# Splitting the second halves of K's and V's weights at later places in the recurrence

## Chip, cores and metric

The kernel runs as one program on one core of a Trainium2 chip. The metric is the device time of one execution in microseconds (us). The kernel before takes 1784.86 us, the median of three runs (1783.5 to 1788.74).

## What is computed

The reference is one inference step of a two-layer encoder over 544 tokens (512 of a prompt, 32 of a sample). Layer 0 is an RWKV-7 layer of 32 heads of 64, layer 1 a stick-breaking attention. The change touches layer 0 alone, cut here to what matters:

```python
h, gate = ada_modulate(x, c, norm_g, ada_w, ada_b)
r, k, v, z = split(concat([h, dx]) @ concat([w_in, w_mu]))      # four projections 1024 -> 2048
def step(s, inp):                                               # per token and head, s is 64 x 64
    s_kk = einsum('bhvk,bhk->bhv', s, kk_t)
    s = s * w_t - s_kk * (kk_t * a_t) + v_t * k_t
    return s, einsum('bhvk,bhk->bhv', s, r_t)
```

The projections K and V are what the moved instructions prepare weights for; the recurrence is computed in chunks of 64 tokens.

## The kernel before

**Tiling.** Activations lie with their features on the 128 partitions and the 544 tokens along the free dimension, in two halves of 272 tokens. A projection of 128 output columns multiplies eight 128x128 weight tiles with eight 128x272 activation tiles for each half. Float32 accuracy comes from splitting every operand into a rounded high part and a low remainder, and from three matmuls per tile (high by high, high by low, low by high).

**Weights.** `wfetch` (L219) loads half of one projection's weights (four of its eight tiles, 256 KB) into one of four raw buffers through the SyncE queue (SP). `wsplit` (L224) makes the high part `whi` by a copy on ScalarE (ACT, L231) and the low part `wlo` by a subtraction (L232), in the recurrence on VectorE (DVE). In the recurrence there are three pairs of `whi` and `wlo` buffers, used in turn; a split waits until the matmuls that read the buffer's last contents are done, and `wlo` waits for `whi`.

**Schedule.** The 2048 features are 16 pairs of heads. While pair p is prepared, pair p-2 runs its recurrence: one unit of the schedule ("an iteration" below) holds the V projection of one pair (places 0 to 0.5), the K projection of another (0.5 to 1), the recurrence of a third, and the vector work of others. The order on every engine is written out by hand: `at(t, fn)` enters a step at a place t, a table `SHIFT` moves some of them by thousandths, and `flush` (L530) issues all steps sorted by place. Each engine runs its own instructions in that order, so one that waits holds up all that stand behind it on the same engine. A projection issues 16 quanta of three matmuls, half by half (`quantum`, L553); 11/32 of an iteration after the start of its slot (less 0.0107 by the table) stands the last quantum that reads the first half of the weights.

**Order of the halves.** Per iteration four halves are split in the order K0, K1 (the K weights for the next slot) and V0, V1. With three buffers, K1 takes the buffer that V0 held, and V1 the one that K0 held. V0 is last read by the quantum at place 0.333, K0 by the one at 0.833; before the change K1 is split at place 0.300 and V1 at 0.800. K0 (0.22) and V0 (0.72) take the buffers of the projections that ended before.

**The chain of the recurrence** (`plan_c`, L887) is in eight steps n per iteration, at places 3n/24 (`x`), (3n+1)/24 (`u`) and (3n+2)/24 (`s`): L907 on TensorE (PE) multiplies the state, L918 copies on DVE, L929 on PE, L932 and L933 copy on ACT, L944 on PE, L952 on DVE makes the new state `st`, and L922 on ACT scales it. Step 2's `st` stands at 0.3333, step 6's at 0.8333. In front of step 2's on DVE stands also L666, which makes `rk`.

**The triangular inverses** (`plan_b`, L730): per iteration GpSimd (POOL) runs 31 pairs of instructions (L771, L776) on one pair of heads, each depending on the one before. Their input goes through DRAM: masks on DVE (L689), stores on SP (L741), loads into `npt` (L754); their result is stored by SP (L757) and fetched back (L745), and DVE transposes it (L791, place 0.86) for the matmuls of L797. On SP these stand in the order L741, L757 (which waits for POOL's last add), L754, L745.

Of the kernel before, what the change touches and what calls it, by code (L numbers as in the profile page):

```python
# [87 lines left out]
def tile_encoder(ctx: ExitStack, tc: tile.TileContext, i, o):  # L88
# [130 lines left out]
    def wfetch(n, kh):  # L219
        raw = wp.tile([P, KH, P], F32, tag="wraw", name="wraw", bufs=RBUF)  # L220
        SY.dma_start(raw, wsrc[n][kh * KH * P:(kh + 1) * KH * P].rearrange("(k p) c -> p k c", p=P))
        return raw

    def wsplit(raw):  # L224

        n, pool = wcount[0] % (WBUF + WMORE if wmore else WBUF), wp
        wcount[0] += 1
        if n >= WBUF:
            pool = wmore[0]
        hi, lo = (pool.tile([P, KH, P], F32R, tag=f"{nm}{n}", name=nm, bufs=1) for nm in ("whi", "wlo"))  # L230
        A.copy(hi, raw)  # L231
        (V if onV[0] else G).tensor_tensor(out=lo, in0=raw, in1=hi.bitcast(F32), op=ALU.subtract)  # L232
        return hi, lo
# [288 lines left out]
    def at(t, fn, *args):  # L522

        names = fn.__qualname__.split(".<locals>.")[1:]
        name = names[-1]
        alike = name in ("row", "add", "quantum", "x", "u", "s") or (name == "y" and args != (8,))
        key = " ".join([layer[0]] + names + [str(a) for a in args if not alike])
        agenda.append((t + SHIFT.get(key, 0.0), len(agenda), fn, args))
# [4 lines left out]
            fn(*args)  # L533
        agenda.clear()

    def plan_load(idx, t, d=0.17):

        parts = wready[idx] = [None, None]

        def load(kh):  # L540
            parts[kh] = wfetch(idx, kh)

        def split_w(kh):
            parts[kh] = wsplit(parts[kh])
        for kh in range(2):
            at(t + 0.3 * d * kh, load, kh)
            at(t + d + 0.47 * d * kh, split_w, kh)

    def plan_proj(x, idx, t0, t1, evac):

# [618 lines left out]
    at(1.02, open_b)  # L1169
    for p, q in enumerate(pairs):  # L1170
        if p >= 2:
            plan_load(q.kw, p - 0.95)
        if p >= 1:
            plan_load(q.vw, p + 0.55)
        for plan in (plan_a, plan_lm, plan_b, plan_m, plan_v, plan_c, plan_d):
            plan(q)

# [162 lines left out]
    for k in range(NK):  # L1340
# [14 lines left out]
        else:  # L1355
            t = p3.tile([P, T], F32, tag="t3", name="sqt", bufs=4)
# [65 lines left out]
    def plan_zb(j, idx, t0, t1):  # L1422

        st = {}

        def evac(half, ps, s):
            if half == 0:
                st["t"] = p4.tile([P, T], F32, tag="szb", name="szb", bufs=2)
            u = p4.tile([P, HT], F32, tag="nsq", name="sgm", bufs=2)
            A.activation(u, ps, AF.Sigmoid)  # L1430
            V.tensor_tensor(st["t"][:, s], ps, u, ALU.mult)
        plan_load(idx, t0 - 0.2, 0.1)
        plan_proj(xb, idx, t0, t1, evac)

        def store():
            SY.dma_start(sz_d[j], st["t"])
        at(t1 + 0.05, store)
# [358 lines left out]
```

## Time and profile before

| What | Value |
|---|---|
| median of 3 runs | 1784.86 us (1783.5 to 1788.74) |
| the profiled execution: time | 1785.67 us |
| the profiled execution: span, first to last instruction | 1784.0 us |
| busy in the span: PE, ACT, DVE, POOL | 94%, 50%, 43%, 38% |
| mean granted TensorE clock | 0.982 of full speed |
| the recurrence, start of its first step to the end of its last | about 256 to 875 us |

The profile is of one execution. Busy shares are of the whole span; the two granted levels of the TensorE clock are 1.2 and 2.4 GHz, and a mean between them is a mix of the two. The recurrence runs in 16 iterations (numbered 2 to 17 by the schedule's places); K1 is split in iterations 2 to 14 and V1 in 2 to 15. An iteration's bounds are taken as the starts of its first L907 matmul on `s`. Times in rows are from the start of the span.

### The profile page before, as it was taken

How to read it: one execution, taken by the hardware profiler on the slowest of the kernel's cores; microseconds unless marked ns; L12 is line 12 of the kernel's file. 1: busy time of each engine (PE TensorE's matmuls, PEld its weight loads, DVE VectorE, ACT ScalarE, POOL GpSimd, SP SyncE). 2: the span in 40 equal slices, each digit the busy share in tenths (PEclk: the TensorE clock that was granted, in tenths of full speed). 3: DMA queues.
4: the chain of work that ended last, by engine and by line, in shares of the span. 5: the costliest groups of instructions: out<-in, count | busy, mean ns of one | idle time of the engine just before them, and what ended most of it. 6: DMA issues, size and time to landing. Idle time of an engine off the chain costs nothing. (4 is left out here: it accounts for less than half of the span.)

```text
span 1784.0 us, 38442 instructions
## 1 busy us (share of the span) xinstructions
PE 1675.3 (94%) x15107; PEld 1444.3 (81%) x15107; DVE 765.6 (43%) x1564; ACT 884.9 (50%) x2232; POOL 681.4 (38%) x1371
## 2 busy tenths in 40 slices
PE   5999979999999999999989998999999999999899
PEld 2679867777777777778868998998888888888798
DVE  3674445545555545552355223123443434334400
ACT  2555545565565556555443335254554545555521
POOL 1000276656667666663002443432222222222432
PEclk8999989999999999989999999999999999999999
DMA  8457522333232333332585443433233232323232
GB/s 326 154 160 233 180 76 69 108 84 86 73 80 73 107 80 93 94 89 66 178 287 148 125 142 91 139 106 110 63 85 88 66 107 58 98 75 103 78 111 79
DMA packets 302612, 203.75 MB, mean 114 GB/s; under 512 B 79726, under 2 KB 271872, under 8 KB 300256
## 3 DMA queue, kind: packets, MB, share of 16 engines
q1 hardware_dynamic: 302432, 201.30, 38.2%
q8 instruction: 119, 1.95, 0.5%
q14 instruction: 61, 0.50, 0.1%
HBM read 155.28 MB, written 45.96 MB: 113 GB/s over the span
## 5 line engine op out<-in xcount | busy, mean ns | idle before, releaser
L560 PE MATMUL mm<-x,whi 128*128 128x272 f32 x3584 | 798.4, 315 | 7.0 <-DVE x L1274 3.5
L560 PEld LDWEIGHTS mm<-x,whi 128*128 128x128 f32 x3584 | 572.0, 191 | 70.7 <-issue 23.3
L232 POOL TENSOR_TENSOR wlo<-wraw,whi 128x512 fp32r<-128x512 f32 x198 | 255.2, 1299 | 702.1 <-ACT whi L231 702.1
L560 PE MATMUL mm<-x,wlo 128*128 128x272 f32 x1792 | 520.8, 291 | 1.7 <-POOL wlo L232 1.7
L560 PEld LDWEIGHTS mm<-x,wlo 128*128 128x128 f32 x1792 | 341.3, 190 | 2.4 <-POOL wlo L232 2.4
L231 ACT CAST whi<-wraw 128x512 fp32r<-128x512 f32 x324 | 195.1, 618 | 138.1 <-issue 78.4
L771 POOL TENSOR_TENSOR qtmp<-npt,qp 108x84 f32<-108x84 f32 (+23 forms) x496 | 194.0, 391 | 77.9 <-DMA npt<-nd_d 38.4
L776 POOL TENSOR_TENSOR qp<-qp,qtmp 108x84 f32<-108x84 f32 (+23 forms) x496 | 194.7, 393 | 37.9
L232 DVE TENSOR_TENSOR wlo<-wraw,whi 128x512 fp32r<-128x512 f32 x126 | 88.9, 707 | 116.3 <-ACT whi L231 114.6
L260 PE MATMUL mm<-x,whi 128*128 128x272 f32 x512 | 101.2, 293 | 2.8 <-POOL x L1733 1.4
L932 ACT COPY vu<-ch 64x64 f32<-64x64 f32 (+1 forms) x128 | 27.5, 215 | 133.7 <-PE ch L929 133.4
L952 DVE SCALAR_TENSOR_TENSOR st<-ch,gc,sgc 128x64 f32<-128x64 f32 x128 | 35.7, 279 | 128.2 <-PE ch L944 125.0
L260 PEld LDWEIGHTS mm<-x,whi 128*128 128x128 f32 x512 | 81.7, 190 | 3.9 <-POOL x L1733 1.8
L560 PE MATMUL mm<-xrh,whi 128*128 128x272 f32 x240 | 73.0, 304 | 1.6 <-ACT rout L1087 1.4
L260 PE MATMUL mm<-x,wlo 128*128 128x272 f32 x256 | 74.5, 291 | 0.0
L260 PE MATMUL mm<-yh,whi 128*128 128x272 f32 x256 | 73.9, 288 | 0.0
L260 PE MATMUL mm<-yh,wlo 128*128 128x272 f32 x256 | 73.8, 288 | 0.0
L260 PE MATMUL mm<-yl,whi 128*128 128x272 f32 x256 | 73.8, 288 | 0.0
L560 PE MATMUL mm<-xrh,wlo 128*128 128x272 f32 x240 | 69.3, 289 | 0.3 <-DVE wlo L232 0.3
L560 PE MATMUL mm<-xrl,whi 128*128 128x272 f32 x240 | 69.1, 288 | 0.0
L922 ACT ACTIVATE sgc<-st,gc 128x64 f32<-128x64 f32 x112 | 38.7, 346 | 46.6 <-DVE st L952 46.2
L1640 ACT ACTIVATE z<-z 128x512 f32<-128x512 f32 (+1 forms) x48 | 27.8, 579 | 68.1 <-DVE z L1637 68.1
(322 smaller groups left out, 3180.0 us busy)
## 6 DMA issues: line engine op xcount, KB each, us to landing
wraw<-in_a_w_in_dram SPq DMA_DIRECT2D x128, 256.0 KB
wraw<-in_kv_w_dram SPq DMA_DIRECT2D x68, 256.0 KB
wraw<-in_b_w_in_dram SPq DMA_DIRECT2D x64, 256.0 KB
rca<-rca_d SPq DMA_DIRECT2D x16, 816.0 KB
rca_d<-sgat SPq DMA_DIRECT2D x16, 544.0 KB
x<-in_a_ada_w_dram SPq DMA_DIRECT2D x8, 1024.0 KB
adaw<-in_b_ada_w_dram SPq DMA_DIRECT2D x8, 1024.0 KB
wraw<-in_a_w_out_dram SPq DMA_DIRECT2D x32, 256.0 KB
```

The source lines that it names most:

```text
L231: A.copy(hi, raw)
L232: (V if onV[0] else G).tensor_tensor(out=lo, in0=raw, in1=hi.bitcast(F32), op=ALU.subtract)
L260: TE.matmul(ps[:, :HT], a[:, k % KH, :], b[:, k, s], start=n == 0, stop=n == total - 1)
L560: TE.matmul(ps[half][:, :HT], a[:, k % KH, :], b[:, k, s], start=k + n == 0, stop=k == NK - 1 and n == 2)
L771: G.tensor_tensor(q.tt, q.npt[:, j, j + 1:32].unsqueeze(1).broadcast_to([108, ni, nt]), q.qp[:, 0:ni, j:j + 1].broadcast_to([108, ni, nt]) ...
L776: G.tensor_tensor(q.qp[:, 0:ni, j + 1:32], q.qp[:, 0:ni, j + 1:32], q.tt, ALU.add)
L922: A.activation(sg, state[c], AF.Copy, scale=q.gc[:, c:c + 1])
L932: A.copy(q.vu[64:128, cs, 0, :], pu[64:128, 0:64 * m].rearrange("p (m t) -> p m t", m=m))
L952: V.scalar_tensor_tensor(new, src, gc, ps["g", c], ALU.mult, ALU.add)
L1640: A.activation(z[b][:, :width[b]], z[b][:, :width[b]], AF.Exp)
```

## The change

`plan_load` gets an optional place for the split of the second half. For K it is p - 0.57 (place 0.43 of the iteration instead of 0.300), for V it is p + 0.895 (0.895 instead of 0.800). The loads, the first halves, the buffers and their order stay, and so do the other layer's calls of `plan_load`, which give no such place.

```diff
-    def plan_load(idx, t, d=0.17):
+    def plan_load(idx, t, d=0.17, second=None):
...
         for kh in range(2):
             at(t + 0.3 * d * kh, load, kh)
-            at(t + d + 0.47 * d * kh, split_w, kh)
+            at(second if kh and second else t + d + 0.47 * d * kh, split_w, kh)
...
         if p >= 2:
-            plan_load(q.kw, p - 0.95)
+            plan_load(q.kw, p - 0.95, second=p - 0.57)
         if p >= 1:
-            plan_load(q.vw, p + 0.55)
+            plan_load(q.vw, p + 0.55, second=p + 0.895)
```

## Rows read from the trace of the kernel before

**Rows 1.** The page: its span, and busy time, share and instructions by engine.
```profile
span 1784.0 us, 38442 instructions
PE 1675.3 (94%) x15107; PEld 1444.3 (81%) x15107; DVE 765.6 (43%) x1564; ACT 884.9 (50%) x2232; POOL 681.4 (38%) x1371
```

**Rows 2.** Stretches (us, busy by engine, PE clock, DMA): iterations 3-14, 10, 11.
```profile
295.75:756.83 461.08, 435.72 (x5515) 347.48 (x5513) 244.00 (x540) 267.42 (x794) 307.64 (x853) 0.99 0.33 85
563.67:603.26 39.59, 37.41 (x466) 29.89 (x464) 20.30 (x45) 22.30 (x68) 26.25 (x73) 0.96 0.31 81
603.26:641.24 37.98, 35.95 (x466) 28.64 (x463) 20.38 (x45) 22.28 (x68) 26.04 (x73) 1.00 0.33 85
```

**Rows 3.** Waits, 256 to 875 us: who for whom, us, times, longest.
```profile
PE ch L907 <- DVE st L952: 21.9, 17, 1.8
...
DVE wlo L232 <- ACT whi L231: 77.6, 44, 3.4
...
ACT whi L231 <- PE mm L560: 11.7, 27, 1.0
```

**Rows 4.** Timeline (start, us, what, [idle before]), iteration 10, K1; last: iteration 11.
```profile
574.34 0.50 DVE L1033 SCALAR_TENSOR_TENSOR yr<-yr,vecb,vs 128x272 f32<-128x272 f32 x1
...
575.41 0.62 ACT L231 CAST whi<-wraw 128x512 fp32r<-128x512 f32 x1 [0.51 <-PE mm L560]
...
575.42 0.34 PE L944 MATMUL ch<-vu,kbt 128*64 128x64 f32 x4
...
576.06 0.86 DVE L232 TENSOR_TENSOR wlo<-wraw,whi 128x512 fp32r<-128x512 f32 x1 [1.22 <-ACT whi L231]
...
576.85 0.86 DVE L666 TENSOR_TENSOR rk<-rca,k 128x544 f32<-128x544 f32 x1
577.63 0.27 DVE L952 SCALAR_TENSOR_TENSOR st<-ch,gc,sgc 128x64 f32<-128x64 f32 x1
...
577.96 0.33 PE L907 MATMUL ch<-st,ar 64*64 64x64 f32 x4 [1.51 <-DVE st L952]
...
617.37 0.33 PE L907 MATMUL ch<-st,ar 64*64 64x64 f32 x4 [1.33 <-DVE st L952]
```

**Rows 5.** Timeline, iteration 10 around V1's split.
```profile
597.03 0.69 DVE L232 TENSOR_TENSOR wlo<-wraw,whi 128x512 fp32r<-128x512 f32 x1 [3.10 <-ACT whi L231]
...
597.60 0.29 PE L560 MATMUL mm<-x,wlo 128*128 128x272 f32 x1
...
597.98 0.33 PE L907 MATMUL ch<-st,ar 64*64 64x64 f32 x4
...
599.33 0.34 PE L797 MATMUL aux<-mt,lm 32*32 32x32 f32 x10 [0.19 <-DVE mt L791]
```

**Rows 6.** Timeline, iteration 11 around place 0.43.
```profile
619.90 0.21 ACT L933 COPY vu<-ch 64x64 f32<-64x64 f32 x1
...
621.17 0.28 DVE L952 SCALAR_TENSOR_TENSOR st<-ch,gc,sgc 128x64 f32<-128x64 f32 x1 [1.06 <-PE ch L944]
...
621.76 0.33 PE L907 MATMUL ch<-st,ar 64*64 64x64 f32 x4
```

**Rows 7.** Timeline of SP and POOL, iterations 10 and 11: issues, first, last.
```profile
588.89 2.51 SPq L757 DMA_DIRECT2D qd_d<-qp  x3
...
626.83 2.52 SPq L757 DMA_DIRECT2D qd_d<-qp  x3
...
596.55 0.24 POOL L771 TENSOR_TENSOR qtmp<-npt,qp 108x31 f32<-108x31 f32 x1 [2.41 <-DMA npt<-nd_d]
...
625.44 0.23 POOL L776 TENSOR_TENSOR qp<-qp,qtmp 108x11 f32<-108x11 f32 x1
...
634.28 0.24 POOL L771 TENSOR_TENSOR qtmp<-npt,qp 108x31 f32<-108x31 f32 x1 [2.19 <-DMA npt<-nd_d]
```

**Rows 8.** The same POOL instruction alone and beside DVE's work, iterations 10, 11.
```profile
566.21 0.34 POOL L771 TENSOR_TENSOR qtmp<-npt,qp 108x84 f32<-108x84 f32 x1
...
604.28 0.73 POOL L771 TENSOR_TENSOR qtmp<-npt,qp 108x84 f32<-108x84 f32 x1
```

## Prediction

> **What bounds the kernel now.** The page comes first: PE is busy 94% of the span and every other engine half of it or less [rows 1], so only a place where PE stands still, or its clock is down, can give time back. Next the view by stretches, cut at the iterations of the recurrence: iterations 3 to 14 last 461.08 us together, of which PE works 435.72; the rest, 25.4 us or 2.1 us per iteration, is what a new order of the vector work could win. Most iterations are like the 11th (37.98 us, clock 1.00); three are like the 10th (39.59 us, clock 0.96) [rows 2]. Then the waits in the recurrence: PE waited 17 times, 21.9 us in all, for the new state `st`. DVE stood 44 times, 77.6 us in all, in a `wlo` for ACT's `whi`, and ACT stood 27 times, 11.7 us in all, in a `whi` until matmuls let go of its buffer [rows 3]. That 27 is the 13 splits of K1 and the 14 of V1 which the change moves.
>
> The timeline of one iteration joins the three. At K1's split ACT stands 0.51 us until the last quantum on the buffer is done, copies for 0.62 us, and DVE, which had stood 1.22 us, subtracts from 576.06. Behind it on DVE stand `rk` (576.85) and step 2's `st` (577.63), although the matmuls that feed `st` ended at 575.42 + 0.34 = 575.76. PE runs out of quanta and stands 1.51 us before L907 in iteration 10, and 1.33 us in iteration 11 [rows 4]. All 13 iterations with a K1 split show this stall, at about one of these two sizes.
>
> **The change, part by part.** Nothing is added: the same two ACT copies and two DVE subtractions run later, and the buffers, the loads and the order of the halves stay. A split issues no DMA; the raw buffers are let go later, but the next load into each comes about an iteration later. SP, POOL and PE keep their programs.
>
> *K1 away from 0.300.* `rk` can follow the instruction before it, at 574.34 + 0.50 = 574.84, and hand DVE on after 577.63 - 576.85 = 0.78 us, at 575.62; so `st` starts when its matmuls allow, about 575.8 by the 575.76 above. L907 followed `st` by 577.96 - 577.63 = 0.33 us, so it could start at 576.13. PE works until 577.96 - 1.51 = 576.45 [rows 4]. The whole stall goes, with 0.3 us to spare: 1.33 us in an iteration like the 11th.
>
> *K1 at 0.43.* It comes on ACT right behind step 3's copies, and on DVE just ahead of step 3's `st`. In iteration 11 the copies end at 619.90 + 0.21 = 620.11; 0.62 for `whi` and about 0.65 for `wlo` to hand DVE on (as short as 0.61, as long as the 0.79 from 576.06 to 576.85 [rows 4]) give 621.38 to 621.5, against 621.17 today. L907 follows at 621.76, and `st` plus 0.33 would then be 621.71 to 621.83 [rows 6]. Cost: 0 to 0.1 us; I take 0, because PE is working on quanta until then. The weights are wanted only at place 0.61, 0.18 x 38 = 7 us later.
>
> *V1 away from 0.800.* DVE stood 3.10 us and then subtracted, but PE worked until 597.60 + 0.29 = 597.89 and L907 started at 597.98: 0.09 us. Behind it DVE reaches the transposes later, and PE waits 0.19 us for them in L797 and splits that group in two [rows 5]. Worth 0.1 to 0.5 us per iteration, 0.3 taken.
>
> *V1 at 0.895.* On ACT it comes ahead of step 7's copies, on DVE ahead of step 7's `st`, while PE is in L797 (599.33) and has step 7's matmuls still before it [rows 5]. Nothing that it would delay is due yet: cost 0, or as K1's place up to 0.1 us. The weights are wanted at 1.11.
>
> Without another limit, an iteration like the 11th would last 37.98 - 1.33 - 0.3 = 36.35 us.
>
> **What is late next.** The inverses make a loop of their own: POOL's last add, SP's store of the result, load of the next input, POOL's first multiply. SP issued the store of iteration 10 at 588.89 and POOL began at 596.55: 7.66 us. POOL then ran until 625.44 + 0.23 = 625.67: 29.12 us. The next store went out at 626.83, and POOL began at 634.28: 7.45 us [rows 7]. So the loop needs 29.12 + 7.45 to 7.66 = 36.6 to 36.8 us, and today's iteration leaves it 626.83 - 625.67 = 1.16 us to spare, because SP gets there from the masks, which follow PE. An iteration of 36.35 us is shorter than the loop. After about two of them the spare time is used up, the fetched inverse comes late to DVE's transposes, and PE waits for it in L797. I therefore take 36.8 us for the iterations after that.
>
> *Sum.* Iterations 3 to 14 last 461.08 us [rows 2]. Afterwards: 2 x 36.35 + 10 x 36.8 = 440.7 us, 20.4 us less. Iteration 2 loses one more K1 stall, 1.4 us as the others, and iteration 15 one V1 wait, 0.3 us: 22.1 us in all. The profiled execution's time is 1785.67 us (span 1784.0 and 1.67 around it), 0.81 above the median: 1784.86 - 22.1 = 1762.8, so **1763 us**, 1.2% below. In this sum the clock stays at its upper level. The three iterations like the 10th lost 39.59 - 37.98 = 1.61 us to a lower clock right behind the 1.51 us stall [rows 2, 4]; 4.8 of the 20.4 us come from there.
>
> **The rivals.**
> *The whole gain comes.* If POOL's loop speeds up a little or the slack behind it is larger than I see, all twelve run at 36.35 us less the upper end for V1 (36.15): 433.8 us, 27.3 less, with 1.7 as above 29 us: 1756. For it: POOL's time depends on what DVE does beside it [rows 8]. Against it: two loops agree within 0.2 us [rows 7].
>
> *The clock still falls.* Three iterations keep a cold stretch: 3 x 1.61 = 4.8 us back, 1768. If the loop also needs 37.1 us, 3 us more: 1771. For it: PE keeps short gaps, and the late inverse makes a new one. Against it: nine of the twelve iterations kept the full clock even with the stall, and without it each has less standing time than those. The Trainium skill (TensorE: Matmul & The Clock Gate, "A second HAM failure mode: psum-queue depth-cycling") holds that frequent small idles between groups of matmuls are enough to make the clock go up and down; by that the falls would stay although the long stall goes, and the time would be this rival's. In the recurrence the trace shows a fall only behind a stall of over a microsecond (1.51 us in iteration 10), so I give it the smaller chance.
>
> *The wait only moves.* If `wlo` at place 0.43 holds step 3's `st` for as long as it now holds step 2's, PE stands there instead and nothing is won: 1780 to 1785. It decides at 0.1 us or more beyond what PE's quanta cover; today's rows leave it within 0.1 us [rows 6], and it would have to grow to 1.3.
>
> *Slower.* POOL's loop becomes longer than the iteration of before. The same POOL instruction took 0.34 us with DVE idle and 0.73 us beside a DVE subtraction or product, 0.39 more [rows 8]. If each moved `wlo` now falls on three POOL instructions that ran freely, 2 x 3 x 0.39 = 2.3 us are added: the loop is 39.1 us, 12 x 39.1 = 469.2 against 461.08, 8.1 us more, less the 1.7 of iterations 2 and 15: 1791. It decides at 1.6 us added to the loop. Against it: both subtractions stand beside POOL's work already, so what is added at the new places is taken away at the old. The Trainium skill (GPSIMD Engine Reference, "8. Key points") says that GpSimd shares its SBUF interfaces with VectorE and is held up by VectorE instructions with two SBUF inputs; `wlo` is one, and the trace agrees (0.73 against 0.34).
>
> **How the numbers follow.** Forecast, 1760 to 1766: 0.50. Whole gain, 1756: 0.18. Clock falls, 1768 to 1771: 0.18. The wait moves: 0.10. Slower: 0.04. The first three hold 0.86, so the range is 1756 to 1771. A measurement of this kernel tells about 0.3% (5.4 us) from no change: faster 0.86, same 0.10, slower 0.04.
>
> **What would show it.** In the profile of after, ACT's waits in `whi` for the matmuls (27, 11.7 us) should be gone, and PE's for `st` fall from 21.9 us to under 5. Iterations 3 to 14 should last 36.3 at first and then 36.6 to 37, with SP waiting for POOL's last add at L757 and PE or DVE waiting for the inverse at L791 and L797; if SP doesn't wait there, the loop isn't what is late next. No stretch of iterations 3 to 14 should have a clock under 0.98. The prediction is wrong if step 3's or step 7's `st` is late behind `wlo`, if POOL's 29.1 us per iteration change by over half a microsecond, or if PE's stall stays at step 2 because `rk` alone holds `st`.

## The result and the profile after

The changed kernel takes 1772.21 us, the median of five runs (1764.21 to 1774.4), against 1788.74 us for the kernel before on the same chips (1783.5 to 1794.77): a ratio of 0.990, 95% interval 0.9864 to 0.9935. Its profiled execution took 1773.3 us (1785.67 before). The forecast was 1763 us, a ratio of 0.988. On the 1784.86 us from which it was worked out, 0.990 is 1767 us: that is nearer to the rival in which the clock falls (1768 to 1771) than to the forecast's own 1760 to 1766. Right were the direction, the rough size, the stall that goes and what is late next; wrong was that the clock stays up, and what V1's move is worth.

The page of after, span and busy time, to be read against [rows 1]:

```profile
span 1771.6 us, 38443 instructions
PE 1677.7 (95%) x15107; PEld 1449.1 (82%) x15107; DVE 765.0 (43%) x1564; ACT 881.3 (50%) x2232; POOL 682.3 (39%) x1371
```

PE's busy time grew by 2.4 us while the span lost 12.4: part of what PE no longer waits, it spends on slower matmuls. Waits of after in the recurrence (257 to 863 us; who for whom, us in total, times, longest), to be read against [rows 3]:

```profile
PE aux L797 <- DVE mt L791: 6.9, 13, 1.6
PE ch L907 <- DVE st L952: 4.7, 4, 1.9
...
SPq L757 <- POOL gc L600: 13.8, 6, 2.4
SPq L757 <- POOL qp L776: 7.7, 3, 5.4
...
DVE mt L791 <- DMA lm<-qd_d: 10.8, 10, 2.2
```

PE's wait for `st` fell from 21.9 to 4.7 us. In its place stands a chain that the kernel before hardly showed: SP waits at L757 for POOL (9 times, 21.5 us; before once, 4.8 us), DVE waits in the transposes for the fetched inverse (10 times), PE waits in L797 for DVE (6.9 us). ACT's wait in a `whi` for matmuls is gone from the list.

The step that stalled before, in iteration 11 of after (start, us, what), against [rows 4 and 6]:

```profile
607.30 0.87 DVE L666 TENSOR_TENSOR rk<-rca,k 128x544 f32<-128x544 f32 x1
607.92 0.34 PE L944 MATMUL ch<-vu,kbt 128*64 128x64 f32 x4
608.38 0.28 DVE L952 SCALAR_TENSOR_TENSOR st<-ch,gc,sgc 128x64 f32<-128x64 f32 x1 [0.20 <-PE ch L944]
...
608.88 0.33 PE L907 MATMUL ch<-st,ar 64*64 64x64 f32 x4
...
611.51 0.62 ACT L231 CAST whi<-wraw 128x512 fp32r<-128x512 f32 x1
612.16 0.74 DVE L232 TENSOR_TENSOR wlo<-wraw,whi 128x512 fp32r<-128x512 f32 x1 [0.54 <-ACT whi L231]
612.22 0.34 PE L944 MATMUL ch<-vu,kbt 128*64 128x64 f32 x4
612.83 0.27 DVE L952 SCALAR_TENSOR_TENSOR st<-ch,gc,sgc 128x64 f32<-128x64 f32 x1
...
613.27 0.33 PE L907 MATMUL ch<-st,ar 64*64 64x64 f32 x4
```

`rk` moved ahead, step 2's `st` follows its matmuls within half a microsecond, and the 1.33 us are gone. At the new place step 3's `st` starts 0.61 us after L944 (621.17 - 620.72 = 0.45 before), and PE still does not stand.

Stretches of after (us, busy by engine, PE clock): iterations 3 to 14 together, then the 3rd, 5th, 9th and 12th, against [rows 2]:

```profile
293.43:745.79 452.36, 441.82 (x5515) 354.01 (x5512) 243.85 (x540) 265.34 (x795) 308.51 (x859) 0.96 0.34 88
293.43:333.82 40.39, 38.24 (x465) 30.75 (x463) 20.29 (x45) 22.63 (x69) 27.79 (x79) 0.93 0.31 80
371.17:407.04 35.87, 35.53 (x465) 28.54 (x463) 20.54 (x45) 22.04 (x68) 24.55 (x70) 1.00 0.34 90
519.20:558.57 39.37, 38.02 (x466) 30.55 (x463) 20.42 (x45) 22.62 (x69) 27.10 (x77) 0.93 0.32 82
632.33:669.62 37.29, 35.81 (x466) 28.66 (x463) 20.36 (x45) 22.04 (x68) 25.63 (x73) 1.00 0.33 87
```

Three kinds can be seen: 35.87 us where nothing is late, 37.29 us where POOL's loop is late and the clock holds, 39 to 40 us where the clock falls as well. Iterations 3 to 14 together became 461.08 - 452.36 = 8.7 us shorter, not 20.4. The other 3.7 us of the span lie around them, where 1.7 were forecast: iteration 2 is 3.5 us shorter, iteration 15 1.1 and what follows 0.3, while the recurrence starts 1.2 later.

### The profile page after: what moved, and what is told of

Same layout as the page of the kernel before. It is cut to its first block, busy times and chain, and to the rows that moved or that the text cites. A ratio compares the mean times of both kernels' runs of the same rounds, so it can differ in the third digit from the quotient of the medians.

```text
span 1771.6 us, 38443 instructions
## 1 busy us (share of the span) xinstructions
PE 1677.7 (95%) x15107; PEld 1449.1 (82%) x15107; DVE 765.0 (43%) x1564; ACT 881.3 (50%) x2232; POOL 682.3 (39%) x1371
## 5 line engine op out<-in xcount | busy, mean ns | idle before, releaser
L689 DVE TENSOR_TENSOR lm<-aux,cmask 128x512 f32<-128x512 f32 (+1 forms) x96 | 49.1, 552 | 26.9 <-PE aux L685 25.7
```

The costliest lines, as they stand in the source:

```text
L689: V.tensor_tensor(q.lm[:, hd, c0:c0 + n].rearrange("p c a t -> p c (a t)"), pp[hd][:, :n * P].rearrange("p (m x) -> p m x", x=P), cmask.re ...
```

## Experiments

Sums are of iterations 3 to 14 of the profiled execution; ratios are to the kernel before, on the same chip, with 95% intervals.

| Run | Ratio | Iterations 3 to 14, us | Clock there |
|---|---|---|---|
| before | 1 | 461.08 | 0.99 |
| the change | 0.990 (0.9864 to 0.9935) | 452.36 | 0.96 |
| K1 alone (e1) | 0.9856 (0.9836 to 0.9877) | 438.53 | 1.00 |
| V1 alone (e2) | 0.9931 (0.9907 to 0.9954) | 455.82 | 0.99 |
| the change, short inverse (e3) | 0.978 (0.976 to 0.980) | 430.84 | 1.00 |
| K1 alone, short inverse (e8) | 0.9835 (0.9814 to 0.9855) | 438.64 | 1.00 |

### K1 alone, V1 alone

```diff
 e1:
-            plan_load(q.vw, p + 0.55, second=p + 0.895)
+            plan_load(q.vw, p + 0.55)
 e2:
-            plan_load(q.kw, p - 0.95, second=p - 0.57)
+            plan_load(q.kw, p - 0.95)
```

> Only K1's split is moved to place 0.43; V1 stays at 0.800. Theory (K1 carries the gain: it takes PE's stall of 1.33 to 1.53 us at step 2 out of 13 iterations, and POOL's loop of about 36.9 us is what is late next): iterations 3 to 14 about as long as with both moves, 37 to 38 us on average; time 0.7 to 1.0% below the kernel before. Rival (the two moves are needed together, V1 carries half): at most 0.5% below. The wait of PE for st in the recurrence should fall from 21.9 us to under 8, and the wait for the inverse (L797) should be smaller than the 6.9 us of the changed kernel, since V1's wlo in front of the transposes gives the fetch more time.

> Only V1's split is moved to place 0.895; K1 stays at 0.300. Theory: PE's stall at step 2 stays (13 times, 1.3 to 1.5 us), an iteration at full clock is 37.98 - 0.3 = 37.7 us, POOL's loop is shorter than that and doesn't bind: 2 to 5 us below the kernel before (0.1 to 0.3%). Rival (V1 carries half): 8 us or more below.

K1 alone did better than either theory said: it is 1.44% below the kernel before, ahead of both moves together. V1 alone is 0.69% below, 10.2 us by the medians. That is more than the theory's 2 to 5 us and meets the rival's number of 8 us; but that V1 carries half doesn't follow, since K1 alone gives more than both. Of the 9.1 us by which V1's move shortened the profiled span (1784.0 to 1774.9), 5.3 lie in iterations 3 to 14. Stretches of K1 alone (iterations 3 to 14, and the 10th), of V1 alone (3 to 14, and the 12th), and the 9th of the kernel before, in that order:

```profile
294.97:733.50 438.53, 430.49 (x5514) 344.11 (x5512) 242.70 (x540) 265.83 (x794) 301.41 (x853) 1.00 0.34 89
550.81:587.36 36.55, 35.87 (x465) 28.67 (x463) 20.21 (x45) 22.15 (x68) 25.06 (x71) 1.00 0.34 88
```

```profile
294.99:750.81 455.82, 432.59 (x5515) 346.76 (x5513) 243.82 (x540) 265.58 (x794) 309.38 (x856) 0.99 0.33 86
638.49:675.92 37.43, 35.59 (x465) 28.55 (x463) 20.42 (x45) 22.14 (x68) 25.45 (x71) 1.00 0.32 87
```

```profile
525.53:563.67 38.14, 35.97 (x465) 28.66 (x463) 20.30 (x45) 22.29 (x68) 25.68 (x71) 1.00 0.33 85
```

With K1 alone every iteration from 3 to 14 lasts 36.5 to 36.6 us, PE works 35.87 of them, and none has a lower clock: the stall of step 2 is gone and nothing takes its place. The timeline of POOL, DVE and PE there shows why (iteration 10; last, POOL's last add of the same inverse):

```profile
581.06 0.24 POOL L771 TENSOR_TENSOR qtmp<-npt,qp 108x31 f32<-108x31 f32 x1 [2.69 <-DMA npt<-nd_d]
581.14 0.70 DVE L232 TENSOR_TENSOR wlo<-wraw,whi 128x512 fp32r<-128x512 f32 x1 [3.09 <-ACT whi L231]
...
582.10 0.33 PE L907 MATMUL ch<-st,ar 64*64 64x64 f32 x4
...
582.42 0.97 DVE L791 STREAM_TRANSPOSE mt<-lm 32x288 f32<-32x288 f32 x2
...
583.03 0.22 PE L797 MATMUL aux<-mt,lm 32*32 32x32 f32 x2
583.44 0.75 PE L797 MATMUL aux<-mt,lm 32*32 32x32 f32 x34 [0.19 <-DVE mt L791]
...
609.55 0.23 POOL L776 TENSOR_TENSOR qp<-qp,qtmp 108x11 f32<-108x11 f32 x1
```

V1's `wlo` still stands ahead of the transposes, which come 582.42 - 550.81 = 31.61 us into the iteration (30.80 with both moves where nothing is late, in e3 below: 571.95 - 541.15). The fetched inverse has landed by then, and DVE does not wait. POOL's loop and PE's iteration are in step. With V1 alone the stall of step 2 stays (PE waited 22.9 us for `st` in the recurrence, 21.9 before). Its 12th iteration and the 9th of the kernel before both hold a stall of 1.5 us there, at the full clock: V1's move made it 38.14 - 37.43 = 0.71 us shorter.

### Is POOL's loop what is late?

```diff
-        for j in range(31):
+        for j in list(range(18)) + list(range(23, 31)):
             at(b0 + (b1 - b0) * (2 * j) / 62, row, j)
```

on the change (e3), on the kernel before (e4) and on K1 alone (e8). Five of the 31 rows of each inverse are left out on POOL, so these three don't compute the reference; they only shorten POOL's loop.

> The changed kernel, with rows 18 to 22 of each triangular inverse left out on POOL (5 of 31 pairs of instructions, about 4 us of POOL's 29.1 per iteration), so that the inverses are not the reference's. Theory (POOL's loop binds after the change, and its late inverse makes the stall at L797 and the falls of the clock): PE no longer waits for the transposes in L797, the clock stays above 0.99 in iterations 3 to 14, each lasts 35.9 to 36.3 us; time 1750 to 1758. Rival (the falls of the clock come from the many short gaps, not from the stall at L797): the iterations keep falling to 0.93 to 0.96 in four or more of twelve, time 1764 or more. Rival (POOL isn't what is late): the same as the changed kernel, 1764 to 1774.

> The kernel before, with the same five rows of each inverse left out on POOL. Theory (before the change POOL's loop has 1 us to spare and the stall at step 2 sets the pace): within 0.3% of the kernel before. Rival (POOL sets the pace already before): 10 us or more below.

> K1's move alone, with rows 18 to 22 of each inverse left out on POOL, so that the inverses are not the reference's. Theory (with K1's move alone PE and not POOL's loop sets the pace): an iteration stays at 36.5 us, within 0.2 us of the kernel with K1's move alone, and 0.65 us longer than with both moves and the short inverse (35.87): that difference is V1's move where nothing else is late. Rival (POOL's loop sets the pace here too): 36.0 us or less.

Stretches of the change and of K1 alone with the short inverse, iterations 3 to 14:

```profile
289.67:720.51 430.84, 426.65 (x5514) 342.76 (x5512) 243.89 (x540) 264.53 (x794) 266.52 (x733) 1.00 0.35 91
```

```profile
289.97:728.61 438.64, 430.58 (x5514) 343.88 (x5512) 242.99 (x540) 265.74 (x794) 263.11 (x731) 1.00 0.34 89
```

With the short inverse the change runs at 430.84 / 12 = 35.9 us per iteration, with no stall at L797 over 0.25 us and the clock up throughout; with the whole one it took 452.36. So 21.5 us of iterations 3 to 14 hang on POOL's loop. K1 alone does not care (438.64 against 438.53): there PE sets the pace. The difference 438.64 - 430.84 = 7.8 us, 0.65 per iteration, is what V1's move is worth where nothing else is late. POOL was also busy longer with both moves than with K1's alone, by 266.52 - 263.11 = 3.4 us here and by 308.51 - 301.41 = 7.1 us in the whole kernels.

The two busy times of PE tell what the 21.5 us are made of: 441.82 - 426.65 = 15.2 us are the same matmuls at a lower clock, the other 6.3 us PE stood. e3's time, 1747.52 us, is a little under the theory's 1750.

The kernel before (e4) came 0.43% lower (0.9957, 0.994 to 0.9973), a little more than the theory allowed. Its iterations 3 to 14 took 458.16 us, 2.9 less, and iteration 2 began at 251.78 instead of 255.84 us: ahead of the recurrence PE waits for the first inverse (5.3 us in L797, 1.2 in e4), which a shorter POOL makes earlier. Those 4 us, more or less, are in e3 and e8 too; the sums of iterations 3 to 14 leave them out. Part of the 2.9 us is the clock: it fell twice there, three times in the kernel before.

### The loop made shorter without leaving work out

The three loads of the next inverse's input stand on SP behind the store of the last one. Issued elsewhere, they need not.

```diff
-            SY.dma_start(q.npt[36 * g:36 * g + 36], nd)
+            G.dma_start(q.npt[36 * g:36 * g + 36], nd)      # e5; e6: A.dma_start
...
-            at(t0 + 0.70, load, g)
+            at(t0 + 0.645, load, g)                         # e9 alone, with G.dma_start
```

> The changed kernel, with the three loads of the next inverse's input issued by POOL itself instead of standing on SP behind the store of the last one. Theory (the loop of POOL's last add, SP's store, SP's load and POOL's first multiply, about 37 us, is what is late, and its lateness makes the stalls at L797 and the falls of the clock): the loop loses SP's 2.7 us before the load, it is 34 to 35 us, shorter than PE's 35.9; PE doesn't wait in L797, the clock stays over 0.99 in iterations 3 to 14, each lasts 35.9 to 36.3 us; time 1748 to 1757. Rival (POOL pays for issuing its own loads with as much as SP's queue cost): POOL starts as late as in the changed kernel, 1764 to 1774.

> The same with the three loads issued by ACT. Theory (the loop is what is late): 1748 to 1757 if ACT isn't held up. Rival (ACT stands in the load until the stores to DRAM have landed, some 2 us, and the copies of the recurrence's steps behind it are late): PE waits in L944 for ACT's copies once per iteration, and the time is 1765 to 1790.

> As the run with the loads issued by POOL, but at place 0.645 instead of 0.70, ahead of POOL's two small copies (L599, L600) that waited 2.9 us per iteration for ACT there. Theory (the loop is what is late, and in the earlier run those copies stood in it): POOL starts 1 to 3 us sooner after its last add than the 7 us of that run, the loop is 33.5 to 35.5 us, iterations 3 to 14 last 35.9 to 36.3 us with the clock over 0.99 and no wait in L797 over 0.3 us; time 1748 to 1756. Rival (POOL's own loads land no sooner, wherever they stand): stalls at L797 and falls of the clock remain, 1764 to 1774.

Issued by POOL, 0.9911 (0.9891 to 0.9932): the rival's time. Issued by POOL earlier, 0.9888 (0.9863 to 0.9913): again the rival's. Iterations 3 to 14 gained a part of it, 444.8 and 446.2 us against 452.36, and in e5 iterations 4 to 9 lasted 35.9 to 36.1 us each, as the theory said; but in both the loop was late again later, and the clock fell twice. Issued by ACT, 0.9826 (0.9808 to 0.9844), 1754.65 us: the theory's. POOL's waits of e5 and of e9, and SP's issues of e9 in iteration 6:

```profile
POOL gc L599 <- ACT gx L593: 34.8, 12, 8.6
POOL qp L764 <- DMA qd_d<-qp: 25.7, 13, 4.7
POOL qtmp L771 <- DMA npt<-nd_d: 17.0, 10, 3.2
```

```profile
POOL npt L754 <- DMA nd_d<-lm: 38.1, 13, 5.2
POOL qp L764 <- DMA qd_d<-qp: 35.5, 13, 4.7
POOL qtmp L771 <- DMA npt<-nd_d: 8.3, 8, 2.8
```

```profile
424.93 2.53 SPq L757 DMA_DIRECT2D qd_d<-qp  x3
430.83 1.81 SPq L745 DMA_DIRECT2D lm<-qd_d  x4
```

In e5 POOL stood in front of its loads for ACT's `gx`. In e9 it did not, but it stood there until the masks' stores had landed (L754), and then until the store of the last result had, before it could clear `qp` (L764). SP's fetch of that result came 430.83 - 424.93 = 5.9 us after the store, 4.3 before (588.89 to 593.20 in iteration 10): loads and stores now run at the same time. POOL's wait for `npt` shrank and the fetch came later, so PE kept its stalls at L797. The gain of e6 rests on its stretch:

```profile
292.50:728.21 435.71, 428.38 (x5515) 342.97 (x5513) 243.03 (x540) 266.36 (x794) 307.53 (x854) 1.00 0.34 90
```

36.3 us per iteration, clock 1.00, its longest stall at L797 0.34 us. It is the shortest kernel of this study that leaves nothing out, and by the ratios it beats the change by 0.7%; its interval still touches that of K1 alone (0.9836 to 0.9877).

### V1 at a third place

```diff
-            plan_load(q.vw, p + 0.55, second=p + 0.895)
+            plan_load(q.vw, p + 0.55, second=p + 0.84)
```

> Both splits are moved, V1 only to place 0.840, behind step 6's st and still ahead of the transposes on DVE. Theory (V1's move hurts because it lets DVE reach the transposes, and PE the next masks, sooner than POOL's loop can follow): an iteration is 36.3 to 36.6 us with the clock over 0.99, nearly as with K1's move alone, and 1756 to 1764. Rival (what hurts is wlo beside POOL's work at any place behind step 6's st): POOL's 62 instructions last 29.1 us or more and the stalls at L797 are there, 1764 to 1774.

Both were wrong: 1.0034 (1.0016 to 1.0052), slower than the kernel before. Timeline of iteration 4:

```profile
361.54 0.28 DVE L952 SCALAR_TENSOR_TENSOR st<-ch,gc,sgc 128x64 f32<-128x64 f32 x1 [2.91 <-PE ch L944]
...
361.95 0.60 ACT L231 CAST whi<-wraw 128x512 fp32r<-128x512 f32 x1
...
362.58 0.69 DVE L232 TENSOR_TENSOR wlo<-wraw,whi 128x512 fp32r<-128x512 f32 x1 [0.76 <-ACT whi L231]
...
363.66 0.97 DVE L791 STREAM_TRANSPOSE mt<-lm 32x288 f32<-32x288 f32 x2
364.27 0.22 PE L797 MATMUL aux<-mt,lm 32*32 32x32 f32 x2 [0.87 <-DVE mt L791]
```

`whi` stands on ACT behind a 0.87 us activation (L609), so `wlo` waits 0.76 us on DVE, and the transposes wait for `wlo`. PE reaches L797 sooner than DVE does and stands 0.85 to 0.94 us in every iteration. No DMA is late here. Iterations 3 to 14 took 466.8 us. With the clock up such an iteration lasts 37.2 us; but in eight of the twelve the clock's mean fell to 0.94 or lower, and they last 38.9 to 41.4 us.

### Both against K1 alone on one chip

Both kernels once more, beside each other.

> The changed kernel once more, beside K1's move alone on one chip. Theory (V1's move costs where POOL's loop is late): 0.3 to 0.7% slower than K1's move alone, with falls of the clock behind stalls at L797 in several of iterations 3 to 14, at other iterations than in its first profile. Rival (the two profiles differ by chance): within 0.2% of K1's move alone.

> K1's move alone once more, beside both moves. Theory: 1757 to 1766, no stall at L797 and the clock over 0.99 in all of iterations 3 to 14, each 36.5 to 36.6 us. Rival (its even run was chance): stalls and falls of the clock as with both moves, 1764 to 1774.

Both moves: 0.990 (0.988 to 0.992). K1 alone: 0.9854 (0.9834 to 0.9874). The intervals don't touch; V1's move on top of K1's costs about 0.5%, 8 us. The profile of both moves shows stalls at L797 of 0.59 to 1.74 us in five iterations, and four spells of low clock in iterations 3 to 14, at partly other iterations than the first time (3, 7, 9, 12; the first time 3, 7, 9, 14). K1 alone missed its expectation in one spot: stalls of 0.45 and 0.62 us at L797 in iterations 3 and 4 and one spell of low clock of 10.2 us behind the second; the other nine iterations last 36.5 to 36.6 us again. Even that kernel's loop has little to spare.

## Why the prediction was right, and where not

**K1 away from 0.300: right.** 1.33 us were forecast per iteration; K1 alone gives 37.98 - 36.55 = 1.4 us, and the chain `rk`, `st`, L907 runs as worked out.

**K1 at 0.43: right.** No PE wait appears at step 3 in iterations 3 to 14.

**V1: the term was mis-sized, and its sign depends on the loop.** 0.3 us was taken, 0.1 to 0.5 as bounds; it measures 0.65 us where POOL is short (e8 against e3) and 0.71 where K1's stall stays (e2). The bounds came from PE's own waits of 0.09 and 0.19 us at two instructions. They left out that L797 would run in one piece: with K1 alone it lasts from 583.03 to 583.44 + 0.75 = 584.19, 1.16 us, in e3 0.76. Step 7's L907 comes 0.19 us sooner as well (31.29 us into the iteration in e1, 31.10 in e3).

```profile
573.08 0.76 PE L797 MATMUL aux<-mt,lm 32*32 32x32 f32 x36
```

Where POOL's loop is late the move gives nothing and costs 0.5% (e10, e11). It works on the loop from both sides: PE's iteration would be 0.65 us shorter, and POOL's 62 instructions of an inverse last longer, 609.55 + 0.23 - 581.06 = 28.72 us with K1 alone in the rows above, 655.83 + 0.23 - 627.07 = 28.99 with both in the rows below; on average over the ten inverses begun in iterations 3 to 12, 28.73 and 29.14 (28.72 and 29.24 in e11 and e10). How much of the cost is either's was not told apart.

**What is late next: right, but it came sooner.** POOL's loop was put at 36.6 to 36.8 us, late after about two iterations; PE's first stall at L797, the longest of all (1.62 us), stands in iteration 3 already. SP and POOL of after, iterations 11 and 12:

```profile
656.09 2.51 SPq L757 DMA_DIRECT2D qd_d<-qp  x3
```

```profile
627.07 0.24 POOL L771 TENSOR_TENSOR qtmp<-npt,qp 108x31 f32<-108x31 f32 x1 [2.75 <-DMA npt<-nd_d]
...
655.83 0.23 POOL L776 TENSOR_TENSOR qp<-qp,qtmp 108x11 f32<-108x11 f32 x1
...
663.99 0.24 POOL L771 TENSOR_TENSOR qtmp<-npt,qp 108x31 f32<-108x31 f32 x1 [2.45 <-DMA npt<-nd_d]
```

POOL ends at 656.06, SP stores 0.03 us later, POOL begins again 7.9 us after that; with 29 us of work the loop is 663.99 - 627.07 = 36.9 us. Iterations 12 and 13, where it is late and the clock holds, last 37.29 and 36.91 us.

**The clock stays up: the step that failed.** The forecast kept it, and priced the falls as a rival at three times 1.61 us, taken from falls behind the stall of step 2. (0.16 of the 1.61 is the longer stall: against the 9th iteration, which has it too, a fall cost 39.59 - 38.14 = 1.45.) The late inverse makes a stall of its own, as the text said PE would have at L797, and the falls behind that one are longer. Stretches of after, the stall of iteration 3 and the fall behind it:

```profile
325.43:327.05 1.62, 0.00 (x0) 0.03 (x1) 0.58 (x2) 0.00 (x0) 0.91 (x5) 1.00 0.61 169
...
327.78:338.01 10.23, 10.23 (x121) 8.31 (x115) 2.83 (x6) 4.17 (x13) 8.51 (x23) 0.50 0.01 2
```

PE works without a pause for 10.2 us at 0.50, the lower of its two levels (1.2 of 2.4 GHz). In iterations 3 to 14 of the kernel before a fall lasted 3.4 us. With ten iterations at 36.8 us the forecast for iterations 3 to 14 was 440.7 us; 452.36 came, 11.7 more. The slower matmuls, 15.2 us against e3, are more than that. But e3 takes away the late loop and the falls together, and in the iteration behind a fall nothing is late (0.2 to 0.4 us of standing in the 4th, 8th and 10th), so what either would cost without the other was not told apart on the chip.

**The rivals.** The whole gain did not come: 433.8 us were its price, 430.84 is what PE alone can do (e3). The wait did not only move: PE does not stand at step 3. The clock's rival did come, beside the loop. The one that ended slower put its price on POOL's contention, 2.3 us per iteration. Against the kernel before POOL's busy time grew by 308.51 - 307.64 = 0.9 us in all twelve, and its 62 instructions last 29.14 us on average against 29.10: in sum what one place adds the other takes away, as the forecast argued. The case that ended slower was another (e7): DVE behind a `wlo` that waits on ACT.

**How near the number came is in part luck.** K1's move alone is worth 1.44% (e1), more than the 1.2% forecast for both. V1's move, forecast as a gain, took 0.5% of it back, through the loop that the forecast had seen and the falls that it had not.

## What to carry to other kernels

A wait taken off the bounding engine is worth its length only until the next loop closes: work out every loop that runs through another engine and the DMA queue, and give each moved instruction a price against that loop, not only against the wait that it ends. Where two loops are within a microsecond, letting one run ahead turns slack into a stall at their meeting point; here one of two moves alone beat both. Move one at a time, and look at the granted clock behind every new stall: a shorter stall at another place can cost more than the one that it replaced (e7).

## What the runs showed of the hardware

The clock fell more often, and for longer, behind a stall at L797 than behind a longer one at step 2. In the kernel before, twelve stalls of 1.33 to 1.53 us (iterations 3 to 14) made three falls of 3.4 us each. In e7, twelve stalls of 0.85 to 0.94 us made five falls of 10.2 us each. One fall of either:

```profile
578.72:582.12 3.40, 3.40 (x33) 2.86 (x32) 1.55 (x4) 0.42 (x2) 2.85 (x10) 0.50 0.59 183
```

```profile
439.95:450.18 10.23, 10.23 (x97) 8.26 (x96) 2.87 (x5) 5.02 (x15) 8.48 (x23) 0.50 0.01 2
```

Counted over iterations 3 to 14 of all profiles: behind step 2's 36 stalls of 1.2 to 1.5 us (before, e2, e4) stand 8 falls, each of 3.4 us. Behind 35 stalls of over 0.4 us at L797 (after, e2, e5, e7, e9, e10, e11) stand 18, of 6.8 or 10.2 us. The four runs with neither kind of stall (e1, e3, e6, e8) have no fall.

Why is open. In the 5 us behind a stall PE runs twelve of the projection's matmuls either way, with 22 of L685's products (64x128) behind step 2's (617.37 in the kernel before) and 72 matmuls of 32x32 behind L797's (327.05 in e7; at both the clock held). That the smaller matmuls are why is argued, not shown: no run changed the work behind a stall while keeping its length. And the place doesn't settle the length of a fall: in iteration 15 a fall of 10.2 us stands behind a stall of 1.8 us at L907 in the kernel before and in e3, and one of 3.4 us behind the same stall in e1.

Loads that were moved to another engine to start earlier went with a later landing of a neighbour: the store that was followed by its fetch after 4.3 us in the kernel before took 5.9 us when the loads ran beside it (e9, iteration 6; 4.9 to 7.6 in the ten inverses of iterations 3 to 12). That the loads are the cause is argued from the order of the issues.
